# Pairing the transposes of a sparse attention's steps and grouping the value products of two memory attentions

## The chip, the core and the metric

The kernel runs on one core of a Trainium2 chip. The metric is device time in microseconds (us), from the first to the last instruction of one execution, as the median of several runs. Five engines work side by side, each through its own queue in order: TensorE (PE; its weight loads are shown apart as PEld), VectorE (DVE), ScalarE (ACT), GpSimd (POOL) and SyncE (SP), which here only issues DMAs. TensorE's results land in PSUM, which this kernel uses as eight banks of 128 x 512 floats; VectorE and ScalarE copy them out.

## What is computed

The reference is a two-layer trunk on one sequence of 512 tokens and width 1024, all in fp32. Layer 0 mixes tokens by a gated linear attention (GLA), layer 1 by a sparse attention (NSA) with three branches: compressed keys, selected blocks, and a window. In both layers a *memory attention* over 256 memory tokens runs beside it, and both are followed by an output projection and a feed-forward network with a short convolution. Cut to what matters here:

```python
def mem_attention(q, mem_kv):                       # 4 heads of 64, 256 memory tokens
    s = einsum("bshd,bmhd->bhsm", qh, kh) * 64 ** -0.5
    return einsum("bhsm,bmhd->bshd", softmax(s), vh)

def nsa_mixer(q, gates, shared, rel_bias):          # 12 heads of 64 in 4 groups
    p_c = masked_softmax(q @ kc.T + bias)           # compressed keys, 31 of them
    o_c = p_c @ vc
    o_s = masked_softmax(q @ k_sel.T + bias) @ v_sel    # selected blocks: all 8 blocks here
    o_w = masked_softmax(q @ kw.T + bias) @ vw          # window of 512
    return g0 * o_c + g1 * o_s + g2 * o_w
```

With 512 tokens there are 8 blocks of 64 and up to 16 may be selected, so the selected branch is causal attention over the whole sequence, like the window.

## The kernel before, in words

Every fp32 product that needs full precision is made of three one-pass products: an operand is split into a high part (ScalarE rounds it to fp32r) and a low part (VectorE subtracts), and high x high, low x high and high x low are summed in PSUM. TensorE's stream is nearly without gaps. A framework places the instructions: each engine's queue follows the program's order, except where an instruction would wait by its own estimate and a later one is free to go first. Where the order matters it is written out by hand: `behind` (L239) ties one instruction behind another on its engine, and in the sparse attention `pe` (L1714) chains all of the stage's matmuls and transposes in program order; only matmuls from outside this chain, such as the output projection's, can still come between.

PSUM is handed out in four pairs of banks, "acc", "sc", "pt" and "po" (`ps`, L209).

**The memory attention** (`mem_att`, L497) works on two pairs of heads, m = 0 and 1, and four tiles of 128 tokens. Ten iterations: iteration i computes the scores of pair and tile i (`scores`, for i under 8), and transposes the weights of i - 2 (`turn`, L521: for each head of the pair two transposes into a "pt" bank, then a copy to the tile mPT, by ScalarE for the first head and VectorE for the second). `fill` puts matmuls of other work in between. When a pair's four tiles are turned, `out` (L534) computes its value products: eight fp32 matmuls of 128 x 64 weights on 512 columns, two heads side by side on the two halves of TensorE's columns, into a "pt" bank, which is then split into mo. Pair 0's products stand in iteration 6, between its scores and its turn (L555), with the split tied between the turn's two copies; pair 1's come after the last iteration (L559).

**The sparse attention** (`nsa_layer`, L1555) has twelve steps: six pairs of heads a = 0..5 (head a with head a + 6), and for each the tiles (0, 3) and then (1, 2) of 128 queries. What belongs to a step:

- `scores` (L1771): for each of the two heads three parts of two matmuls. VectorE adds the bias and takes the minimum, ScalarE exponentiates into the tile P, and after the third part GpSimd multiplies P by gate over sum.
- `copies` (L1889): a DMA from SP's queue copies the finished P to R, from where TensorE reads it in one pass. P and R have three buffers each.
- `weights_t` (L1901): six parts, three for each head. A part is 2 to 4 transposes of R into one bank (mostly "pt", the second branch of a large tile into "acc" up to step 7) and one copy to PT, by ScalarE or VectorE.
- `values` (L1921): 20 fp32 matmuls of PT with V, two heads side by side on half the columns each, into a "po" bank; after tile 2 two more on full columns add the compressed branch, from its transposed weights PcT.
- `compressed` (L1805): the compressed branch for a pair of heads, in four portions: scores on half columns and softmax, multiplication by the gate, transposes of Pc with the copies to PcT.
- `project` (L1724): the query projection of pair a + 2, 24 matmuls, two for each slot of two steps; there is none from step 8 on.

The loop at the end runs over the steps, and each step has six slots (`for i in range(6)`, L1958). A slot s, i issues: a part of the scores of step s + 1, one part of the transposes (half a step behind, so the first three slots finish step s - 1 and the others begin step s), the copies that are due, and two matmuls of the projection. Slot 3 of the even steps 2 to 10 adds, ahead of that: the last portion of the compressed branch (Pc's transposes), the next one's first portion, and the values of the two steps before. Step 11 has no scores and no projection.

Of the kernel before, what the change touches and what calls it, by code (L numbers as in the profile page):

```python
# [18 lines left out]
S = 512  # L19
# [163 lines left out]
class Trunk:  # L183
# [313 lines left out]
    def mem_att(self, qfs, pool, mK, mV, mo, first, fill, qpool, direct=False):  # L497

        nc = self.nc
        Q, P, PT = {}, {}, {}  # L500

        def scores(m, qt):
            ts = slice(128 * qt, 128 * qt + 128)
            sc = self.ps("sc")
            for hh in range(2):
                for i in range(2):
                    ins = nc.tensor.matmul(sc[:, MEM * hh:MEM * hh + MEM], Q[m][hh][i][:, ts], mK[2 * m + hh], start=i == 0, stop=i == 1)
                    if direct:
                        self.behind(ins, self.last)
            mn = self.t(self.small, [128, 2], "mmn")  # L510
            nc.vector.tensor_reduce(out=mn, in_=sc.rearrange("p (h k) -> p h k", h=2), op=ALU.min, axis=AX.X)
            p = P[m, qt] = self.t(pool, [128, 2, MEM], "mP", bufs=3)
            sm = self.t(self.small, [128, 2], "msm")
            for hh in range(2):
                nc.scalar.activation(p[:, hh, :], sc[:, MEM * hh:MEM * hh + MEM], AF.Exp, bias=mn[:, hh:hh + 1], scale=-1.0,
                                     accum_out=sm[:, hh:hh + 1])
            nc.vector.reciprocal(sm, sm)
            for hh in range(2):
                nc.vector.tensor_scalar_mul(p[:, hh, :], p[:, hh, :], sm[:, hh:hh + 1])

        def turn(m, qt, between=None):  # L521
            ts = slice(128 * qt, 128 * qt + 128)
            if qt == 0:
                PT[m] = [self.t(pool, [128, 2, S], f"mPT{hh}", bufs=1) for hh in range(2)]
            for hh in range(2):
                pt = self.ps("pt")
                for kt in range(2):
                    nc.tensor.transpose(pt[:, 128 * kt:128 * kt + 128], P[m, qt][:, hh, 128 * kt:128 * kt + 128], self.ident)
                eng = nc.vector.tensor_copy if hh else nc.scalar.copy
                ins = eng(PT[m][hh][:, :, ts], pt[:, :256].rearrange("p (k t) -> p k t", k=2))  # L530
                if between and hh == 0:
                    between(ins)

        def out(m):  # L534

            po = self.ps("pt")
            for kt in range(2):
                for hh in range(2):
                    g = 2 * m + hh
                    nc.tensor.matmul(po[64 * hh:64 * hh + 64, :], mV[:, kt, 64 * g:64 * g + 64], PT[m][hh][:, kt, :], start=kt == 0, stop=kt == 1)  # L540
            def parts(after=None):
                self.split_to(mo[m][0], mo[m][1], po)
                if after is not None:
                    self.behind(self.made, after)

            return parts

        Q[0] = self.stack_q(qfs[0], pool, qpool, direct)
        first()
        for i in range(10):  # L550
            if i < 8:
                scores(*divmod(i, 4))
            if i == 3:
                Q[1] = self.stack_q(qfs[1], pool, qpool)
            between = out(0) if i == 6 else None  # L555
            if i >= 2:
                turn(*divmod(i - 2, 4), between)
            fill()
        out(1)()  # L559


    def gla_layer(self):
# [992 lines left out]
    def nsa_layer(self):  # L1555
        nc, I, tc = self.nc, self.I, self.tc
        with ExitStack() as outer:
            pool = outer.enter_context(tc.tile_pool(name="nsa", bufs=1))
# [10 lines left out]
            with tc.tile_pool(name="nsap", bufs=2) as pp:  # L1569
# [70 lines left out]
                for j in range(2):  # L1640
# [44 lines left out]
                    else:  # L1685
# [7 lines left out]
                        for g in range(4):  # L1693
                            hh = g // 2
# [29 lines left out]
            def project(a):  # L1724

                wh, wl = self.wget(self.W["nsaq"][a], GMIX)
                ps = self.ps("acc")
                for k in range(KC):
                    ws = slice(128 * k, 128 * k + 128)
                    xh, xl = self.x[k]  # L1730
                    for i, (u, w) in enumerate(((wh, xh), (wl, xh), (wh, xl))):
                        mm(ps, u[:, ws], w, start=k + i == 0, stop=k == KC - 1 and i == 2)
                        if k < KC - 1 or i < 2:
                            yield
                qfs_[a] = self.t(qp, [128, S], "qf", bufs=2)
                nc.vector.scalar_tensor_tensor(out=qfs_[a], in0=ps, scalar=-0.125, in1=rb, op0=ALU.mult, op1=ALU.mult)
                yield
# [101 lines left out]
            run = lambda g, n=1: [next(g, None) for _ in range(n)]  # L1839

            with ExitStack() as ms:
# [6 lines left out]
                def values():  # L1848
                    pv = [self.ps("acc" if t < 2 else "po") for t in range(4)]
                    yield from self.stepsB("nsav", 0, 2, 512, pv, self.x, GKV)  # L1850
                    for t in range(4):
                        nc.scalar.activation(V[:, t], pv[t].rearrange("p (a d) -> p a d", d=64), AF.Copy, scale=rc[:, t:t + 1])
# [30 lines left out]
            with tc.tile_pool(name="nsac", bufs=2) as cp:  # L1883
# [5 lines left out]
                def copies():  # L1889

                    while scaled:
                        s, hh, flat = scaled.pop(0)
                        a, qts = steps[s]
                        direct = s == 11 and hh == 1
                        R = flat if direct else self.t(cp, [128, 1280], "R", FR, bufs=3)
                        for sp, t in zip(spans[qts], qts):
                            if not direct:
                                nc.sync.dma_start(R[:, sp].bitcast(F32), flat[:, sp])
                            Ps[a, t, hh] = by_branch(R[:, sp]), F32 if direct else FR
# [45 lines left out]
                def turns():  # L1945
                    for s in range(12):
                        yield from weights_t(s)

                copies()
                now = turns()  # L1950
                main = [None] * 6 + mo
                for s, (a, qts) in enumerate(steps):
                    ahead = scores(s + 1) if s < 11 else iter(())
                    if qts[0] == 0:
                        proj = project(a + 2) if a < 4 else iter(())
                        q = queries(a + 1) if a < 5 else iter(())
                        run(q)
                    for i in range(6):  # L1958
                        if i == 3 and s and not qts[0]:
                            run(c)  # L1960
                            c = compressed(a)
                            run(c)
                            run(values(s - 2))
                            run(values(s - 1))
                        if i == 4 and s == 11:
                            run(c)
                            run(values(10))
                        if a < 5 and i in (3, 4) and not qts[0]:
                            run(q)
                        if i == 5 and s and not qts[0]:  # L1970
                            run(c)
                        if a < 5 and not i and qts[0]:
                            run(q, 2)
                        run(ahead)
                        if s or i > 2:
                            run(now)
                        copies()
                        run(proj, 2)
                    if 8 <= s < 11:
                        main[s - 8] = self.split(o[s - 8], self.xp, [128, S], "x")  # L1980
                        self.behind(self.made, turned[True])
                        self.behind(self.left, turned[False])
                run(now, 3)
                run(values(11))
            self.w_out(1, main)

# [25 lines left out]
```

## Time and profile before

| | before |
|---|---|
| median of 3 runs (lowest to highest) | 1220.11 us (1219.74 to 1221.58) |
| the profiled execution | 1219.85 us, span 1218.1 us |
| instructions | 22021, of these 8321 matmuls |
| memory attention of layer 0, last fill to last products | up to about 111 us |
| memory attention of layer 1 | up to about 706 us |
| loop of the sparse attention | about 709 to 824 us |

A line of the profile names the line of the kernel, the engine, the operation, out<-in by the program's names, shapes and count; in a timeline the first number is the start in us from the start of the span and the second how long it was busy. TensorE's rows overlap, since its matmuls are pipelined, so their cost is read from start to start. `idle before <-X` names what an engine waited for.

### The profile page before, as it was taken

The page shows a single profiled execution, that of the slowest core. Times are in us where ns is not written, and L with a number is a line of the kernel's source. Part 1 is how long each engine was busy: PE and PEld are TensorE (multiplying, and loading weights), DVE is VectorE, ACT ScalarE, POOL GpSimd, SP SyncE. Part 2 cuts the span into 40 slices and gives each one's busy share as a digit, 9 for nine tenths or more (in the row PEclk, how much of TensorE's full clock was granted, in tenths as well). Part 3 has the DMA queues.
Part 4 walks back from the last instruction along what each step waited for, and adds up shares of the span by engine and source line. Part 5 has one row for each costly group of instructions (what it writes and reads, how often), then busy time and mean ns, then how long its engine had stood idle before and what let it go on. Part 6 is the DMA issues. An engine that isn't in the chain of part 4 may idle for free.

```text
span 1218.1 us, 22021 instructions
## 1 busy us (share of the span) xinstructions
PE 1209.1 (99%) x8321; PEld 1077.6 (88%) x8321; DVE 916.3 (75%) x1637; ACT 729.9 (60%) x1459; POOL 271.0 (22%) x290
## 2 busy tenths in 40 slices
PE   9999999999999999999999999999999999999998
PEld 8887889889999998888888888888899999998887
DVE  7667886698888889644776788975788888889431
ACT  8656655467666667333545678763576666685331
POOL 1000000014444420000003265650034444400000
PEclk9999999999999999999999999999999999999999
DMA  7541013236666642322725467733256666633221
GB/s 263 156 139 60 36 37 105 102 104 171 158 158 156 156 124 90 122 92 98 223 105 173 115 227 249 234 116 121 81 141 160 156 157 156 157 105 108 104 70 69
DMA packets 59776, 163.09 MB, mean 134 GB/s; under 512 B 7309, under 2 KB 13384, under 8 KB 59670
## 3 DMA queue, kind: packets, MB, share of 16 engines
q1 hardware_dynamic: 47638, 140.66, 34.1%
q0 software_dynamic: 10944, 19.93, 10.8%
q8 instruction: 65, 1.06, 0.4%
q10 hardware_dynamic: 1088, 1.10, 0.3%
q14 instruction: 41, 0.34, 0.1%
HBM read 116.13 MB, written 2.15 MB: 97 GB/s over the span
## 4 chain that ended last, share of the span: by engine, by line
PE 92%; DVE 2%; POOL 2%; issue 2%; ACT 1%; DMA 1%; SPq 0%; POOLq 0%; DVEq 0%; ACTq 0%
PE pt L1190 18%; PE acc L326 10%; PE po L1190 9%; PE acc L1423 7%; PE acc L1007 6%; PE po L1362 5%; PE sc L1362 5%; PE sc L1190 5%; PE po L346 3%; PE acc L793 3%; PE po L1721 2%; PE acc L1486 2%; PE acc L1721 2%; PE acc L1627 2%; PE acc L346 2%
## 5 line engine op out<-in xcount | busy, mean ns | idle before, releaser
L287 ACT ACTIVATE wh<-wraw 128x1024 fp32r<-128x1024 f32 (+1 forms) x105 | 109.3, 1042 | 138.9 <-PE sc L1362 29.6
L288 DVE TENSOR_TENSOR wl<-wraw,wh 128x1024 fp32r<-128x1024 f32 (+1 forms) x105 | 130.7, 1246 | 74.2 <-ACT wh L287 73.4
L1179 DVE TENSOR_TENSOR wl<-wraw,wh 128x1024 fp32r<-128x1024 f32 x76 | 72.6, 955 | 7.4 <-ACT wh L1176 7.4
L326 PE MATMUL acc<-xh,wh 128*128 128x512 f32 x184 | 72.6, 394 | 0.0
L326 PE MATMUL acc<-xl,wh 128*128 128x512 f32 x184 | 71.9, 391 | 0.0
L326 PE MATMUL acc<-xh,wl 128*128 128x512 f32 x184 | 71.9, 391 | 0.0
L1423 PE MATMUL acc<-a,wh 128*128 128x512 f32 x228 | 71.2, 389 | 0.0
L1170 POOL DMA_DIRECT2D wraw<-rbw x38 | 33.4, 879 | 154.4 <-DVE wl L1179 111.0
L1179 DVE TENSOR_TENSOR wl<-rbw,wh 128x1024 fp32r<-128x1024 f32 x38 | 46.5, 1225 | 25.9 <-ACT wh L1176 25.9
L1176 ACT ACTIVATE wh<-wraw 128x1024 fp32r<-128x1024 f32 x76 | 63.9, 844 | 1.2 <-DMA wraw<-rbw 1.2
L1060 DVE SCALAR_TENSOR_TENSOR hc<-acc,ntap,hc 128x511 f32<-128x511 f32 x76 | 56.9, 749 | 10.1 <-ACT hc L1057 8.2
L1801 POOL TENSOR_TENSOR P<-P,ssm 128x256 f32<-128x256 f32 (+3 forms) x48 | 61.7, 1306 | 1.9
L1060 DVE SCALAR_TENSOR_TENSOR hc<-acc,vec,hc 128x511 f32<-128x511 f32 x76 | 56.9, 749 | 2.9 <-ACT hc L1057 1.7
L1793 ACT ACTIVATE P<-P,smn 128x128 f32<-128x128 f32 (+3 forms) x96 | 53.3, 557 | 6.5 <-DVE smn L1791 3.2
L1362 PE MATMUL po<-a,wh 128*128 128x512 f32 x144 | 56.0, 389 | 0.0
L1362 PE MATMUL sc<-a,wh 128*128 128x512 f32 x144 | 56.0, 389 | 0.0
L1165 POOL TENSOR_TENSOR rbw<-s,rbw 128x512 f32<-128x512 f32 x36 | 47.8, 1329 | 36.7 <-DVE xh L1068 19.0
L1176 ACT ACTIVATE wh<-rbw 128x1024 fp32r<-128x1024 f32 x38 | 40.3, 1059 | 22.8 <-issue 19.7
L1423 PEld LDWEIGHTS acc<-a,wh 128*128 128x128 f32 x228 | 42.8, 188 | 8.9
L1176 ACT ACTIVATE wh<-s 128x512 fp32r<-128x512 f32 x38 | 24.0, 632 | 42.4 <-PE pt L1190 42.4
L1159 POOL TENSOR_TENSOR s<-wraw,rbw 128x512 f32<-128x512 f32 x34 | 44.8, 1316 | 20.2 <-DVE wl L1179 20.2
L1423 PE MATMUL acc<-a,wl 128*128 128x512 f32 x114 | 44.3, 389 | 0.0
(726 smaller groups left out, 4330.4 us busy)
## 6 DMA issues: line engine op xcount, KB each, us to landing
wraw<-in_wp SPq DMA_DIRECT2D x156, 512.0 KB, 3.2
rbw<-in_wp SPq DMA_DIRECT2D x38, 512.0 KB, 4.4
rbw<-rbw POOLq DMA_DIRECT2D x38, 256.0 KB, 4.2
wraw<-rbw POOLq DMA_DIRECT2D x38, 256.0 KB, 3.3
R<-P SPq DMA_DIRECT2D x12, 512.0 KB, 3.3
strip<-vecd SPq DMA_DIRECT2D x12, 448.0 KB, 4.8
R<-P SPq DMA_DIRECT2D x11, 384.0 KB, 3.0
qd<-qf SPq DMA_DIRECT2D x24, 128.0 KB, 3.2
```

The costliest lines, as they stand in the source:

```text
L287: self.made = nc.scalar.activation(wh, raw, AF.Copy)
L288: self.left = nc.vector.tensor_tensor(out=wl, in0=raw, in1=wh.bitcast(F32), op=ALU.subtract)
L326: self.last = self.nc.tensor.matmul(ps[:M, :N], u[:, M * k:M * k + M], x[k][i][:, :N], start=n == 0, stop=n == 23)
L346: self.last = nc.tensor.matmul(ps[:, :N], s_, m_, start=k == 0 and n == 0, stop=k == KC - 1 and n == 2)
L1007: self.nc.tensor.matmul(ps[:, cols], a[:, o], b[:, cols], start=start and i == 0 and k == ks[0], stop=stop and k == 5 and i == 2)
L1060: return [nc.vector.scalar_tensor_tensor(out=c[:, 2 - i:], in0=u[:, :S - 2 + i], scalar=tap(half, j, i, neg), in1=c[:, 2 - i:], op0=ALU.mu ...
L1176: return after("A", nc.scalar.activation(out, x, AF.Copy))
L1179: return after("D", nc.vector.tensor_tensor(out=out, in0=x, in1=hi.bitcast(F32), op=ALU.subtract))
L1190: after("P", nc.tensor.matmul(bank[:, :256], w[:, o], x, start=start and k + i == 0, stop=k == 3 and i == 2, skip_group_check=True))
L1362: after("P", nc.tensor.matmul(first[m], a[:, o], x, start=r + i == 0, stop=r == NJ - 1 and i == 2))
L1423: nc.tensor.matmul(ps, a[:, o], x, start=n == 0, stop=n == 3 * NJ - 1)
L1801: nc.gpsimd.tensor_tensor(out=P, in0=P, in1=f[:, i, :].unsqueeze(2).to_broadcast([128, 2, 128 * t + 128]), op=ALU.mult)
```

## The change

In `mem_att` the products of pair 0 are taken out of iteration 6 and put behind the last iteration, ahead of those of pair 1; then both are split. The tile mPT gets two buffers, since both pairs are now kept to the end.

In the loop of the sparse attention:

- the transposes run two parts at a time, in the slots 0, 2 and 4 (in step 0 only slot 4; in step 11 also slot 5) instead of one part in every slot, so two are left for the end instead of three;
- in slot 3 of the even steps the values of step s - 2 go ahead of the compressed branch's portions, instead of behind them, and in step 11 those of step 10 do;
- the copies from P to R are not issued in the last slot of a step any more but in the first of the next.

```diff
-                PT[m] = [self.t(pool, [128, 2, S], f"mPT{hh}", bufs=1) for hh in range(2)]
+                PT[m] = [self.t(pool, [128, 2, S], f"mPT{hh}", bufs=2) for hh in range(2)]
...
-            between = out(0) if i == 6 else None
             if i >= 2:
-                turn(*divmod(i - 2, 4), between)
+                turn(*divmod(i - 2, 4))
             fill()
-        out(1)()
+        for part in [out(m) for m in range(2)]:
+            part()
...
                         if i == 3 and s and not qts[0]:
+                            run(values(s - 2))
                             run(c)
                             c = compressed(a)
                             run(c)
-                            run(values(s - 2))
                             run(values(s - 1))
                         if i == 4 and s == 11:
+                            run(values(10))
                             run(c)
-                            run(values(10))
...
                         run(ahead)
-                        if s or i > 2:
-                            run(now)
-                        copies()
+                        if i in (0, 2, 4) and (s or i > 2) or i == 5 and s == 11:
+                            run(now, 2)
+                        if i < 5:
+                            copies()
                         run(proj, 2)
...
-                run(now, 3)
+                run(now, 2)
                 run(values(11))
```

## The prediction, made before the changed kernel was run

> **What bounds the kernel now.** I read the page first (busy shares, slices, the chain), then busy time by stage, then TensorE's rows in order of time around the two places that the diff edits, and last who TensorE waited for in the sparse attention.
>
> ```profile
> span 1218.1 us, 22021 instructions
> PE 1209.1 (99%) x8321; PEld 1077.6 (88%) x8321; DVE 916.3 (75%) x1637; ACT 729.9 (60%) x1459; POOL 271.0 (22%) x290
> ```
>
> TensorE is busy for 1209.1 of 1218.1 us. A time saved on another engine is worth nothing unless TensorE waits for it; a time saved or added in TensorE's own stream counts in full. In the sparse attention the other engines are close behind:
>
> ```profile
> 724.00:744.00 20.00, 19.61 (x186) 16.89 (x183) 17.01 (x52) 15.31 (x47) 11.80 (x17) 1.00 0.73 249
> 783.00:804.00 21.00, 20.39 (x190) 16.93 (x188) 19.37 (x57) 17.11 (x53) 12.86 (x17) 1.00 0.63 210
> ```
>
> The columns are length, then busy PE, PEld, DVE, ACT, POOL, granted clock (1.00), DMA share, GB/s. In the later stage, where no projection runs any more, VectorE is busy for 19.37 of 21 us. So work that bunches there can make TensorE wait. It waits little today (window 705 to 826):
>
> ```profile
> PE sc L1721 <- DVE smn L1791: 0.5, 1, 0.5
> PE acc L1721 <- ACT PT L1917: 0.4, 1, 0.4
> PE pt L1722 <- ACT PT L1917: 0.2, 1, 0.2
> PE acc L1007 <- ACT xh L301: 0.2, 1, 0.2
> ```
>
> That is 1.3 us, and the most that the waits listed there can give back. The sum is made against the profiled execution, 1219.85 us (1.75 us of it outside the span of 1218.1); the median of the runs shown, 1220.11, is 0.26 higher.
>
> **Part 1: two parts of a step in one run of transposes.** A part is 2 to 4 transposes between scores and two projection matmuls. What does a run cost?
>
> ```profile
> 733.93 0.40 PE L1721 MATMUL sc<-K,Ql 128*128 128x512 f32 x1
> 734.16 0.46 PE L1722 MATMUL pt<-ident,R 128*128 128x128 f32 x4
> 734.46 0.47 PE L1721 MATMUL acc<-xl,wh 128*128 128x512 f32 x1
> 734.77 0.39 PE L1721 MATMUL acc<-xh,wh 128*128 128x512 f32 x1
> ...
> 819.55 0.45 PE L1722 MATMUL pt<-ident,R 128*128 128x128 f32 x3
> 819.84 0.43 PE L1722 MATMUL sc<-ident,R 128*128 128x128 f32 x3
> 820.10 1.08 PE L1722 MATMUL pt<-ident,P 128*128 128x128 f32 x7
> ```
>
> Starts count, not busy times, which overlap. A run of four holds TensorE from 734.16 to 734.46, 0.30 us, and the matmul behind it takes 0.31 (734.46 to 734.77) where a 512-column matmul takes 0.23 (733.93 to 734.16): 0.61 in all, of which 0.08 is lost behind the run. One would save that 0.08 with each pair joined, if the transposes kept their pace. They do not: in the one long run of before the second three take 0.26 (819.84 to 820.10), 0.087 each, against 0.30 / 4 = 0.075 in the run of four. Joined, four and four cost 0.61 + 4 x 0.087 = 0.96, and the matmul that lost its run 0.23: 1.19, against 2 x 0.61 = 1.22. The gain is 0.03 us a pair, 0.02 if the rows' rounding falls the other way.
>
> How many pairs: up to the loop's step 10 there are 63 parts in 63 runs now (three in step 0, six in each of the next ten) and 62 parts in 31 runs after. In step 11 no scores or projection stand between the parts, so nothing is joined that wasn't next to each other. 31 pairs x 0.02 to 0.03 give 0.6 to 0.9 us; I take **-0.8 us**.
>
> **Part 2: one group of value products in each memory attention.** The products of pair 0 now stand between the scores and the turns of iteration 6. First the GLA layer's iterations 5 and 6, then the other layer's:
>
> ```profile
> 93.93 0.28 PE L507 MATMUL sc<-mK,Qh 128*128 128x256 f32 x1
> ...
> 96.91 0.28 PE L507 MATMUL sc<-mK,Qh 128*128 128x256 f32 x1
> 97.03 0.28 PE L507 MATMUL sc<-mK,Ql 128*128 128x256 f32 x1
> 97.14 0.28 PE L507 MATMUL sc<-mK,Qh 128*128 128x256 f32 x1
> 97.27 0.28 PE L507 MATMUL sc<-mK,Ql 128*128 128x256 f32 x1
> 97.47 1.94 PE L540 MATMUL pt<-mPT,mV 128*64 128x512 f32 x8
> ...
> 102.27 0.28 PE L507 MATMUL sc<-mK,Qh 128*128 128x256 f32 x1
> ...
> 681.72 0.28 PE L507 MATMUL sc<-mK,Qh 128*128 128x256 f32 x1
> ...
> 685.38 0.28 PE L507 MATMUL sc<-mK,Qh 128*128 128x256 f32 x1
> ...
> 691.13 0.28 PE L507 MATMUL sc<-mK,Qh 128*128 128x256 f32 x1
> ```
>
> ```profile
> 97.96 0.14 PEld L540 LDWEIGHTS pt<-mPT,mV 128*64 128x64 f32 x2 [0.29 <-issue]
> 98.39 0.14 PEld L540 LDWEIGHTS pt<-mPT,mV 128*64 128x64 f32 x2 [0.29 <-issue]
> ```
>
> The products go in pairs of half the array's columns, a pair every 0.43 us (97.96 to 98.39), so four pairs are worth 1.72. Iteration 6 is longer than iteration 5 by (102.27 - 96.91) - (96.91 - 93.93) = 5.36 - 2.98 = 2.38 us in the first layer, and by 5.75 - 3.66 = 2.09 in the second, with the same filling matmuls. What goes beyond 1.72 is 0.66 and 0.37: the price of going into the half-array products and out again, and of a turn that finds one of its two banks taken. At the end of the attention pair 1 stands in such a group already; pair 0, put in front of it, pays 1.72 and no second way in and out. That is **-1.03 us**. The two splits of pair 0 move to the end with it; the first of them runs while pair 1's products take their 1.72 us, and the larger PT buffer is no instruction. If that cover is gone, the splits delay the next stage's use of the banks by some tenths.
>
> **Part 3: step values ahead of the compressed branch.** This edit is easily read as a mere exchange. In the steps 2, 4, 6, 8 and 10, now: Pc transposes, compressed scores, products of step s-2, products of step s-1, all but the transposes on half arrays. After: products of s-2, Pc transposes, compressed scores, products of s-1. TensorE goes into the half-array form twice where it went once.
>
> ```profile
> 745.09 4.54 PE L1721 MATMUL po<-PT,V 128*64 128x128 f32 x80
> 749.56 0.74 PE L1721 MATMUL po<-PcT,vcz 128*128 128x512 f32 x2
> ...
> 817.21 2.41 PE L1721 MATMUL po<-PT,V 128*64 128x128 f32 x40
> ```
>
> Going in costs 0.20 instead of 0.12 (97.27 to 97.47 against 97.03, 97.14, 97.27): 0.08. Eighty rows that follow other half-array work take 4.47 with one way out, forty with a way in and a way out 2.34 (817.21 to 819.55), 0.105 more than half, which is half a way out and a slow first pair: with 0.1 for the way out (estimated from the 0.08 of the way in) 0.05 for the pair, 0.15 together. The three transposes behind take 0.29 where three take 0.26: 0.03. Sum 0.26; part 2 gave 0.37 for the cheaper of its two stays. I take 0.30 x 5 = **+1.5 us**, with 1.3 and 1.9 as ends.
>
> The Trainium skill, "TensorEngine Tiling (Array Packing)", section "Key Properties", says that a change of tiling mode, not of tile alone, drains TensorE; this speaks against part 3 and for part 2, and the rows agree that something is paid at each change. "TensorE: Matmul & The Clock Gate", section "Single matmul latency", puts a drain at about 175 ns, and by that estimate a stay costs 0.35 and the sum would come 0.2 us higher; the rows above show about 0.1 at each change with the rest on the matmuls behind.
>
> **What costs nothing.** The copies to R of the last slot go out one slot later, past the next step's queries and strips on SP's queue; they are used a whole step (six slots of some 1.2 us, and more with the products) later, and wait for GpSimd's scaling anyway. In step 11 the products of step 10 go ahead of the compressed branch with as many ways in and out as before. Without that slack a copy would be late by one slot, about 1.2 us, once.
>
> **Waits.** Two copies out of a run now follow each other on ScalarE and VectorE. Below, the gain is bounded by 2.2 us; above, by the two slower rivals. I take 0: all engines do the same work, and the copies have their step's length to be read.
>
> Sum: -0.8 - 1.03 + 1.5 = -0.33 us, so 1219.85 - 0.33 = 1219.5 for the profiled execution and 1219.8 by the median. 0.2%, 2.4 us, is about what a measurement of this kernel can tell from no change (its three runs lie 1.84 apart). **The forecast is no change that can be told.** Chance 0.57.
>
> **Rivals.** *Slower: the compressed branch's transposed weights come late.* Between the Pc transposes and the products with vcz only one step's products are left as cover.
>
> ```profile
> 723.23 0.60 PE L1722 MATMUL pt<-ident,Pc 128*64 128x128 f32 x4
> 727.07 0.69 DVE L1836 TENSOR_TENSOR PcT<-pt,PcT 64x512 fp32r<-64x512 f32 x1
> 728.75 0.73 PE L1721 MATMUL po<-PcT,vcz 128*128 128x512 f32 x2
> ...
> 804.23 0.60 PE L1722 MATMUL pt<-ident,Pc 128*64 128x128 f32 x4
> ```
>
> ```profile
> 806.16 0.68 DVE L1836 TENSOR_TENSOR PcT<-pt,PcT 64x512 fp32r<-64x512 f32 x1
> ```
>
> Cover now: 723.23 to 728.75, 5.52 us; after, less half of 4.47: 3.3. PcT was there 4.53 us after the transposes began in step 2 (727.07 + 0.69) and 2.61 in step 10. If VectorE's lag stays, step 2 would wait 1.2, step 10 not; with 0.6 as the mean, five steps cost 3.0, and the sum is +2.7: 1222.8. It decides from a lag over 3.3. For it: both engines run behind TensorE here. Against it: the lag is a queue of scores and copies, and the products now put ahead give it 2.2 us to drain; with a drained queue, as in step 10, PcT is in time. Chance 0.15.
>
> *Slower: a bank comes back too late.* With pairs, the bank of part 0 is wanted by part 3 two slots later instead of three.
>
> ```profile
> 736.29 0.28 PE L1721 MATMUL sc<-K,Qh 128*128 128x256 f32 x1
> 736.52 0.46 PE L1722 MATMUL pt<-ident,R 128*128 128x128 f32 x4
> ...
> 739.76 0.40 PE L1721 MATMUL sc<-K,Qh 128*128 128x512 f32 x1
> ```
>
> ```profile
> 738.75 0.66 DVE L1917 COPY PT<-pt 128x512 f32<-128x512 f32 x1
> ```
>
> Three slots take 3.47 us (736.29 to 739.76), two 2.3, and with part 2's transposes ahead 2.6; VectorE had that bank copied 2.9 after its transposes began (738.75 + 0.66 - 736.52). 0.3 short in each of some ten steps: +3, in all 1222.8. Against it: this is one of the longest lags, and a step that waits once lets the copies catch up. Chance 0.07.
>
> *Faster: the waits go.* The pairs leave every second slot without a turn, and the two engines may catch up there. Besides the 1.3 listed, the three turns of step 11 that follow within 4 us may lose less to the banks, for which I allow 0.9. Then -0.33 - 2.2 = -2.5: 1217.6. For it: the waits stand at copies out of banks. Against it: VectorE's 19.37 of 21 us do not shrink. Chance 0.17.
>
> *The change does not do what it says.* Only TensorE's chain of this stage is written out by hand; w_out's matmuls fill gaps from step 8 on and can still part a pair. A third of the pairs undone costs 0.3 us: still no change. Chance 0.04.
>
> **How the numbers follow.** Faster by over 0.2%: the faster rival (0.17) and 0.02 of the forecast's tail, 0.19. Slower: 0.22 of the two rivals less the half of their outcomes below 1222.5 (0.07), and 0.04 of the forecast's tail, 0.19. The rest, 0.62, within 0.2%. The forecast's own range is 1218.5 to 1221.5; that of 8 in 10 reaches into the rivals, 1217.2 to 1222.8.
>
> **What would show it.** Right: in the changed trace runs of six to eight transposes at about 0.087 each, one matmul of 0.30 behind each run; the memory attentions' products x16 in one row, and the iterations 6 of equal length with the others; products x40 on both sides of the Pc transposes, each with 0.2 before its first row. Wrong: TensorE idle ahead of po<-PcT with VectorE's PcT as releaser (first rival), idle ahead of pt<-R with PT copies as releaser (second), or fewer than 0.5 us of listed waits (third). A run of eight at 0.06 each would overturn part 1.

## The result, and the profile after

The changed kernel takes 1227.24 us (median of 6 runs, 1227.0 to 1229.25); the kernel before took 1221.54 beside it (6 runs, 1219.74 to 1221.78). The ratio is 1.0054, with a 95% interval of 1.0044 to 1.0064: slower by half a per cent. The forecast, 1219.8 and no change, was wrong.

The page of the changed kernel (its profiled execution took 1227.06 us):

```profile
span 1225.3 us, 22032 instructions
PE 1211.8 (99%) x8321; PEld 1080.4 (88%) x8321; DVE 917.8 (75%) x1637; ACT 730.4 (60%) x1459; POOL 278.7 (23%) x290
```

The span grew by 7.2 us, TensorE's busy time by 2.7 only, VectorE's by 1.5 and GpSimd's by 7.7, although all of them run the same work. So one looks for waits first: who TensorE waited for in the sparse attention (window 690 to 840).

```profile
PE sc L1721 <- DVE smn L1791: 2.0, 1, 2.0
PE pt L1722 <- ACT PT L1917: 1.6, 3, 0.7
PE sc L1721 <- DVE Ql L302: 0.8, 1, 0.8
PE acc L1007 <- ACT xh L301: 0.7, 1, 0.7
PE acc L1722 <- ACT PT L1917: 0.3, 2, 0.2
PE po L1721 <- DVE PcT L1836: 0.2, 1, 0.2
```

5.6 us, where the list of before had 1.3. (smn is VectorE's minimum over a part of the scores, taken by the instruction that empties the bank of scores; Ql is VectorE's subtraction that makes the low part of a query.) The longest wait has a consequence that no list of waits shows. The same stretch by windows (length, then busy PE, PEld, DVE, ACT, POOL, granted clock, DMA share, GB/s):

```profile
792.00:796.00 4.00, 2.74 (x16) 2.09 (x16) 2.99 (x8) 1.08 (x3) 2.06 (x4) 1.00 0.76 268
796.00:800.00 4.00, 3.25 (x16) 2.66 (x17) 3.75 (x17) 4.00 (x13) 1.60 (x4) 0.79 0.76 244
800.00:804.00 4.00, 4.00 (x23) 3.36 (x21) 4.00 (x5) 2.57 (x9) 2.35 (x2) 0.78 0.30 115
804.00:808.00 4.00, 4.00 (x28) 3.24 (x26) 3.77 (x16) 3.88 (x14) 2.67 (x3) 1.00 0.23 83
```

Behind the wait TensorE's clock is granted at 0.79 and 0.78 of full speed over four us each: (0.21 + 0.22) x 4 = 1.7 us lost. In this execution the waits beyond those of before and the clock are together 4.3 + 1.7 = 6.0 of the 7.2. What the slow clock is worth in the median is not shown: another of the six executions had a mean granted clock of 0.999 (0.997 in the profiled one, 0.998 to 1.0 in those of the kernel before) and took 1227.0 us all the same. Where the long wait comes from stands in VectorE's rows of that place, step 8:

```profile
789.73 1.35 DVE L302 TENSOR_TENSOR Ql<-qd,Qh 128x512 fp32r<-128x512 f32 x1 [0.72 <-ACT Qh L301]
791.11 0.68 DVE L1836 TENSOR_TENSOR PcT<-pt,PcT 64x512 fp32r<-64x512 f32 x1
791.82 0.66 DVE L1817 TENSOR_TENSOR Pc<-sc,strip 128x124 f32<-128x124 f32 x2
792.52 0.41 DVE L1820 TENSOR_REDUCE cmn<-Pc 128x8 f32<-128x248 f32 x1
792.96 0.99 DVE L1821 TENSOR_TENSOR Pc<-Pc,cmn 128x248 f32<-128x248 f32 x1
794.90 0.42 DVE L1826 TENSOR_REDUCE cf<-Pc 128x8 f32<-128x256 f32 x1 [0.94 <-POOL Pc L1824]
795.23 0.42 DVE L1791 CUSTOM_DVE_ANT_0 P<-sc,strip 128x256 f32<-128x256 f32 x1
```

TensorE issued the scores for that last row at 792.41. VectorE was then still at the compressed branch, whose sum cf has to wait for ScalarE's exponential and GpSimd's mask, and the row that would free the "sc" bank stands behind cf in VectorE's queue: it starts 2.82 us after its scores. In the kernel before the same row started 1.53 after them (790.79, scores at 789.26):

```profile
790.19 0.42 DVE L1826 TENSOR_REDUCE cf<-Pc 128x8 f32<-128x256 f32 x1 [0.27 <-POOL Pc L1824]
790.64 0.20 DVE L1827 RECIPROCAL cf<-cf 128x8 f32<-128x8 f32 x1
790.79 0.42 DVE L1791 CUSTOM_DVE_ANT_0 P<-sc,strip 128x256 f32<-128x256 f32 x1
```

Two durations in the changed rows are odd as well: Ql at 1.35 us, where all ten took 0.68 to 0.76 before, and Pc<-Pc,cmn at 0.99, where the same instruction took 1.65 before.

### The profile page after: what moved, and what is told of

It is laid out like the page before. It is cut to its first block, busy times and chain, and to the rows that moved or that the text cites. A ratio compares the mean times of both kernels' runs of the same rounds, so it can differ in the third digit from the quotient of the medians.

```text
span 1225.3 us, 22032 instructions
## 1 busy us (share of the span) xinstructions
PE 1211.8 (99%) x8321; PEld 1080.4 (88%) x8321; DVE 917.8 (75%) x1637; ACT 730.4 (60%) x1459; POOL 278.7 (23%) x290
## 4 chain that ended last, share of the span: by engine, by line
PE 94%; DVE 2%; ACT 2%; issue 1%; DMA 0%; POOL 0%; SPq 0%; POOLq 0%; DVEq 0%; ACTq 0%
PE pt L1190 18%; PE acc L326 11%; PE po L1190 9%; PE acc L1423 7%; PE acc L1007 6%; PE po L1362 5%; PE sc L1362 5%; PE sc L1190 5%; PE po L346 3%; PE acc L793 3%; PE po L1721 2%; PE acc L1486 2%; PE acc L346 2%; PE acc L1627 2%; PE acc L1721 2%; PE sc L1007 1%
## 5 line engine op out<-in xcount | busy, mean ns | idle before, releaser
L1801 POOL TENSOR_TENSOR P<-P,ssm 128x256 f32<-128x256 f32 (+3 forms) x48 | 67.2, 1420 | 1.9
```

The costliest lines, as they stand in the source:

```text
L1801: nc.gpsimd.tensor_tensor(out=P, in0=P, in1=f[:, i, :].unsqueeze(2).to_broadcast([128, 2, 128 * t + 128]), op=ALU.mult)
```

## The experiments

Two theories to begin with. *Late branch*: the new order of slot 3 starts the next compressed branch later and does the harm. *Bunched copies*: two copies out of banks in a row hold TensorE. Times are medians, and ratios are to the kernel before, measured beside each of four groups of experiments (its medians were 1220.67, 1220.83, 1221.07 and 1221.09).

### The parts of the change, one by one

The memory attentions' edit alone (its lines of the diff above, nothing in the loop):

```diff
-            between = out(0) if i == 6 else None
...
+        for part in [out(m) for m in range(2)]:
+            part()
```

> The memory attentions' edit alone. Both theories, late branch and bunched copies, leave this part as I priced it: about 1.0 us faster than before, between 0.6 and 1.3. If it is not faster, the priced way in and out of the half-array products is wrong, or something behind the attention pays it back.

1220.09 us, ratio 0.9994 (0.9985 to 1.0003): 0.6 less, at the lower end of what was expected, and not to be told from no change.

The pairs with the moved copies, in the old order of slot 3:

```diff
-                        if s or i > 2:
-                            run(now)
-                        copies()
+                        if i in (0, 2, 4) and (s or i > 2) or i == 5 and s == 11:
+                            run(now, 2)
+                        if i < 5:
+                            copies()
...
```

> The turns in pairs with the copies of the last slot issued one slot later; slot 3 in its old order. Late branch (the order of slot 3 does the harm): between 0.8 us faster and 0.8 us slower than before, no halved clock. Bunched copies (two PT copies in a row hold banks too long): at least 4 us slower, with waits on PT copies ahead of transposes in most steps.

1227.96 us, ratio 1.0061 (1.0048 to 1.0073).

The new order of slot 3 and step 11 alone:

```diff
+                            run(values(s - 2))
                             run(c)
                             c = compressed(a)
                             run(c)
-                            run(values(s - 2))
...
```

> The order of slot 3 (and of step 11) alone, one part of the transposes in each slot as before. Late branch: 4 to 7 us slower than before, 1.5 of it the five extra stays in half-array form, the rest TensorE waiting for VectorE behind the compressed branch, with a stretch of halved clock. Bunched copies: 1.5 us slower, from the stays alone, and no new wait.

1225.25 us, ratio 1.004 (1.0028 to 1.0053). The time is in the range of *late branch*, but its stretch of halved clock isn't there: every window of this stage is granted full clock. The waits that are new in its list are spread: 0.8 us for Ql, 0.7 for PcT, 0.3 for cf.

The changed kernel without the new order (the first two edits together):

```diff
-                            run(values(s - 2))
                             run(c)
                             c = compressed(a)
                             run(c)
+                            run(values(s - 2))
...
```

> The whole change without the new order of slot 3 and step 11. Late branch: 0.2 to 1.8 us faster than before, at least 5 us faster than the changed kernel. Bunched copies: 3 us or more slower than before. If the two edits add, it is the sum of the two runs that have one of them each.

1226.15 us, ratio 1.0045 (1.0032 to 1.0057).

The memory attentions are innocent. The pairs alone cost 7.3, the order alone 4.6, all of it together about 6. Costs of TensorE's own work would add; waits can cover each other. Neither theory can be the whole: *late branch* had nothing for the pairs, *bunched copies* only 1.5 for the order. In the kernel with the pairs alone, TensorE waits for other things (window 690 to 840; its first four rows):

```profile
PE sc L1721 <- DVE Ql L302: 2.1, 2, 1.2
PE sc L1721 <- ACT PT L1917: 1.0, 1, 1.0
PE pt L1722 <- DVE ssm L1795: 0.8, 1, 0.8
PE acc L1007 <- ACT xh L301: 0.7, 1, 0.7
```

Ql is qd - Qh. All rows of it (minimum, median, maximum in ns), first in the kernel before, then with the pairs:

```profile
L302 DVE TENSOR_TENSOR Ql<-qd,Qh x10: 678/691/761, 709.8 to 795.2; 128x512 fp32r<-128x512 f32 x10
```

```profile
L302 DVE TENSOR_TENSOR Ql<-qd,Qh x10: 691/1084/1952, 710.3 to 801.3; 128x512 fp32r<-128x512 f32 x10
```

And GpSimd at the place of the longest, 801.34 (1.95 us):

```profile
799.82 2.92 POOL L1801 TENSOR_TENSOR P<-P,ssm 128x512 f32<-128x512 f32 x2
```

The subtraction ends at 803.29, 0.55 after GpSimd's scaling of P ended at 802.74. It looks held until the scaling is over. That gave a third theory, *held subtractions*: a VectorE instruction with both inputs in SBUF, and GpSimd's scaling of P, hold each other.

The Trainium skill, "SBUF — State Buffer", section "SBUF: two separate sides", says just this: VectorE and GpSimd share a pair of ports, an instruction of VectorE with two SBUF inputs needs it, and the loser waits for the whole instruction of the other. The runs with a short scaling, below, agree: every Ql takes 0.68 to 0.72 us there, and every Pc<-Pc,cmn 0.41 to 0.42.

### Copies, and GpSimd's scaling cut short

The pairs with the copies to R issued in every slot again:

```diff
-                        if i < 5:
-                            copies()
+                        copies()
```

> The pairs alone, on the kernel before, with the copies to R issued in all six slots as before. Theory 'held subtractions': VectorE's subtractions with both inputs in SBUF (Ql, xl) take 0.69 us when GpSimd is idle and up to 1.95 when its scaling of P runs, since the two hold each other; the pairs shift VectorE against GpSimd, and the copies to R are not the cause: 1225 to 1228. Theory 'late copies': the copies of slot 5, a slot late, keep a P buffer taken and VectorE waits for it (1.88 us in step 1 of the pairs with moved copies, 0.43 before): with them in slot 5 again the loss goes, 1220 to 1222. Theory 'bunched copies': two copies out of banks in a row hold TensorE: as with the moved copies, 1227 to 1228.

1228.07 us, ratio 1.0051 (1.0037 to 1.0064), as slow as with the moved copies. These cost nothing, as forecast, and *late copies* falls.

The kernel before, with GpSimd scaling only 8 columns of each part of P, which leaves out most of the scaling; VectorE's, ScalarE's and TensorE's instructions keep their order. A kernel with this edit is called its *short form*:

```diff
-nc.gpsimd.tensor_tensor(out=P, in0=P, in1=f[:, i, :].unsqueeze(2).to_broadcast([128, 2, 128 * t + 128]), op=ALU.mult)
+nc.gpsimd.tensor_tensor(out=P[:, :, :8], in0=P[:, :, :8], in1=f[:, i, :].unsqueeze(2).to_broadcast([128, 2, 8]), op=ALU.mult)
```

> The kernel before, with GpSimd scaling only the first 8 columns of each part of P instead of all 128 to 512 (the remaining weights are left unscaled); every other instruction is in its old order. It is the base for the next two. All theories: little of GpSimd's time is on the path of the kernel before (1.5 us of waits in this stage): 1219 to 1221. Held subtractions would show all Ql, xl and Pc subtractions at their short times, 0.69 and 0.42 us.

1219.43 us, ratio 0.9986 (0.9977 to 0.9994). The five subtractions Pc<-Pc,cmn, first with full and then with short scaling:

```profile
L1821 DVE TENSOR_TENSOR Pc<-Pc,cmn x5: 1561/1648/1667, 727.8 to 807.3; 128x248 f32<-128x248 f32 x5
```

```profile
L1821 DVE TENSOR_TENSOR Pc<-Pc,cmn x5: 417/418/420, 727.9 to 806.7; 128x248 f32<-128x248 f32 x5
```

So the kernel before was held too, 5 x 1.23 = 6.2 us of VectorE's time, at a place where TensorE was not waiting for it. In the changed kernel four of these five are free (0.42) and the holding falls on Ql, which TensorE waits for (0.8 us in its list):

```profile
L302 DVE TENSOR_TENSOR Ql<-qd,Qh x10: 654/933/1951, 708.4 to 800.9; 128x512 fp32r<-128x512 f32 x10
```

The changed kernel and the pairs with the same edit:

```diff
-nc.gpsimd.tensor_tensor(out=P, in0=P, ...
+nc.gpsimd.tensor_tensor(out=P[:, :, :8], in0=P[:, :, :8], ...
```

> The changed kernel with the same short scaling. Held subtractions: what is left of the change is TensorE's own pace (stays in half-array form +1.5 to +2, pairs 0 to -0.8, memory attentions -1) and some waits at copies, so at most 2.5 over the short form of the kernel before: 1219.5 to 1222.5. Bunched copies: the waits at PT copies (2.6 us) and their consequences stay: 4 or more over it, 1223.5 to 1227. Late branch: the compressed branch's chain still comes late and TensorE waits about 2 us behind it in step 8: 3 or more over it.

> The pairs with the moved copies (1227.96 with full scaling), with the same short scaling. Held subtractions: of the 7.3 us at most 2 are left over the short form of the kernel before: 1219 to 1222. Bunched copies: 5 or more are left: 1225 to 1228.

The changed kernel: 1223.57 us, 4.1 over the short form of before (ratio 1.0017, 1.0009 to 1.0026, to the kernel before itself). The pairs: 1221.59, 2.2 over it (1.0008, 0.9999 to 1.0016). In the pairs with short scaling every Ql is short again:

```profile
L302 DVE TENSOR_TENSOR Ql<-qd,Qh x10: 681/690/702, 710.7 to 796.8; 128x512 fp32r<-128x512 f32 x10
```

GpSimd's long scalings are behind 5.1 of the pairs' 7.3 us, and behind some 2 of the changed kernel's 6. The edit takes away two things at once, the holding and the time for which cf and the weights queue behind the scalings on GpSimd, so the 5.1 is the price of both. In the pairs *bunched copies* missed (5 or more left was expected, 2.2 were left). In the changed kernel *held subtractions* missed (at most 2.5 left was expected, 4.1 were left): something else is there.

### Late banks

The kernel before and the pairs again, and now with the copies out of the banks cut short too, to 8 columns each (PT's other columns stay zero, by four memsets that aren't shown). These are the *light forms*:

```diff
-                                copied = eng(PT[:, brs[0]:brs[-1] + 1, :], pt[...])
+                                copied = eng(PT[:, brs[0]:brs[-1] + 1, :8], pt[...][:, :, :8])
...
```

> The kernel before with the short scaling and with copies of transposed weights out of the banks of only the first 8 columns of each part (the other columns of PT stay zero, four memsets more on GpSimd). The base for the next one. Copies hold TensorE for 0.5 us at most in the kernel with the short scaling alone (1219.43): 1218 to 1220.

> The pairs with moved copies, with the same short scaling and short copies. What is left is TensorE's own pace. Theory 'late banks' (the second part of a run finds its bank still waiting for its copy; of the 2.2 us that the pairs cost over the short form, all is this): the 40 transposes between two compressed branches go from 3.3 to 3.6 us to 3.15, and the pairs gain what was forecast, 0.4 to 0.8 us, against the light form of the kernel before: 1217.3 to 1219.5. Theory 'slow transposes' (a long run is slow in itself): the transposes stay above 3.3 us and the pairs stay 1.5 to 2.5 slower than the light form.

1217.77 us for the light form of before (ratio 0.9971, 0.9961 to 0.9982), 1217.5 for the pairs (0.997, 0.9959 to 0.9982): the pairs' last 2.2 us are gone. The 0.3 us that they are ahead is less than *late banks* expected and can't be told from nothing. The edit also takes time off ScalarE and VectorE, which do the copies, so the price of late banks isn't separated from that. One run, in slot 2 of step 4, first in the pairs with short scaling and full copies, then in the light pairs:

```profile
744.57 0.37 PE L1722 MATMUL pt<-ident,R 128*128 128x128 f32 x3
745.10 0.45 PE L1722 MATMUL acc<-ident,R 128*128 128x128 f32 x3 [0.16 <-ACT PT L1917]
745.38 0.47 PE L1721 MATMUL acc<-xh,wl 128*128 128x512 f32 x1
```

```profile
743.39 0.37 PE L1722 MATMUL pt<-ident,R 128*128 128x128 f32 x3
743.61 0.46 PE L1722 MATMUL acc<-ident,R 128*128 128x128 f32 x3
743.90 0.46 PE L1721 MATMUL acc<-xh,wl 128*128 128x512 f32 x1
```

The run takes 0.81 us instead of 0.51, and only 0.16 of these 0.30 is listed as a wait: the first three transposes are shown as busy for 0.37, although the next part starts 0.22 behind them where it needn't wait. Waits of this kind are found from start to start, not in the list. The same run loses 0.3 us in the steps 2 and 6 too. The copy it waits for, on ScalarE of the first of the two kernels:

```profile
743.60 0.50 ACT L1793 ACTIVATE P<-P,smn 128x256 f32<-128x256 f32 x1
744.10 0.50 ACT L1793 ACTIVATE P<-P,smn 128x256 f32<-128x256 f32 x1
744.59 0.46 ACT L1917 COPY PT<-acc 128x384 f32<-128x384 f32 x1
```

It empties the "acc" bank of the run that began at 742.19, 2.4 us after its start, since it stands behind exponentials.

With full scaling more runs are late. The one in slot 0 of step 5 takes 1.04 us in the pairs (755.93 to 756.97), but 0.46 with short scaling alone (755.33 to 755.79). In the pairs its copy stands behind three exponentials, the first of which had itself to wait; below, that exponential and the wait of the transposes:

```profile
754.76 0.51 ACT L1793 ACTIVATE P<-P,smn 128x256 f32<-128x256 f32 x1 [1.38 <-DMA R<-P]
...
756.77 0.37 PE L1722 MATMUL pt<-ident,R 128*128 128x128 f32 x2 [0.38 <-ACT PT L1917]
```

So late banks are in the 5.1 us of the short scaling as well.

### The late branch

cf and what follows it on VectorE tied behind the two score parts that come next after the branch's block (the fourth and fifth part of the next step), in the changed kernel:

```diff
-                                nc.vector.tensor_tensor_reduce(out=P[:, br, :n], ...
+                                self.scored = nc.vector.tensor_tensor_reduce(out=P[:, br, :n], ...
...
-                nc.vector.tensor_reduce(out=f, in_=Pv, op=ALU.add, axis=AX.X)
+                self.behind(nc.vector.tensor_reduce(out=f, in_=Pv, op=ALU.add, axis=AX.X), self.scored)
```

> The changed kernel, with one order more: in each compressed branch the sum over Pc (cf) and what follows it on VectorE stands behind the first two score parts of the next step instead of ahead of them. In step 8 of the changed kernel VectorE waits for GpSimd ahead of cf, the scores wait behind it, TensorE waits 2.0 us and then runs 3.4 us at half clock. Theory 'late branch': the wait and the slow clock go, 3 us or so less: 1223 to 1225. Theory 'held subtractions alone': the Ql ahead of it is held all the same and the wait only changes its name: 1226 to 1228.

1223.93 us, ratio 1.0021 (1.0013 to 1.003): 3.3 less than the changed kernel. The long wait is shorter, and no window of this stage is granted less than full clock:

```profile
793.82 0.36 PE L1721 MATMUL sc<-K,Qh 128*128 128x256 f32 x1 [1.35 <-DVE smn L1791]
```

The order alone with short scaling (the edit of before's short form), and with the tie and full scaling (the edit just shown):

```diff
+                            run(values(s - 2))
                             run(c)
...
-nc.gpsimd.tensor_tensor(out=P, in0=P, ...
+nc.gpsimd.tensor_tensor(out=P[:, :, :8], in0=P[:, :, :8], ...
```

> The new order of slot 3 and step 11 alone, with GpSimd's short scaling; base is the short form of the kernel before, 1219.43. The block of products, Pc transposes and compressed scores took 6.27 us in the new order against 6.08, so five blocks are worth 0.95. Theory 'late branch': besides that, the compressed branch's chain starts 2.2 us later on VectorE and its cf holds the next scores: 1221.4 to 1223. Theory 'held subtractions': without GpSimd's long scalings nothing but the 0.95 is left: 1220.2 to 1220.8.

> The new order alone, full scaling, with cf tied behind the first two score parts (the order alone took 1225.25, 4.6 over the kernel before). Late branch: the tie takes 1.5 to 3 of it, 1222 to 1223.8. Held subtractions alone: the loss stays, 1224.5 to 1226.

1222.74 us with short scaling (ratio 1.0016, 1.0007 to 1.0025), 3.3 over the short form of before: GpSimd's scalings are only the smaller part of the order's loss. 1222.29 with the tie (ratio 1.0011, 1.0002 to 1.002), 3.0 less than without. Both as *late branch* had it. What is left of the order's cost then is 1.2.

The tie in the old order, alone and with the memory attentions' edit:

```diff
...
+                self.behind(nc.vector.tensor_reduce(out=f, in_=Pv, op=ALU.add, axis=AX.X), self.scored)
...
```

> The kernel before with nothing but the tie of cf. The tie with the memory attentions' edit took 1219.05, the edit alone 1220.09. If the two add: 1219.3 to 1220.0, and the edit is worth 0.5 to 1 with the tie as well. If the tie is worth nothing by itself: 1220.5 to 1221.2.

> The kernel before with the memory attentions' edit alone, and the same tie of cf behind the first score parts. If a late cf holds the scores in the old order too (0.47 us of wait in step 8, 0.1 to 0.3 in others): 0.3 to 0.8 less than the memory edit alone, 1219.3 to 1219.8. If cf is not on the path there: 1220.0 to 1220.6.

1220.33 us alone (ratio 0.9995, 0.9986 to 1.0004) and 1219.05 with the edit (0.9984, 0.9975 to 0.9993). The second beats both kernels, by 2.0 us on the kernel before, a little more than was expected; the wait of 0.5 us for smn is no longer in its list. The tie alone cannot be told from no change.

### What is left without waits

The whole change with short scaling, short copies and the tie:

```diff
+                self.behind(nc.vector.tensor_reduce(out=f, in_=Pv, op=ALU.add, axis=AX.X), self.scored)
...
+nc.gpsimd.tensor_tensor(out=P[:, :, :8], in0=P[:, :, :8], ...
...
+                                copied = eng(PT[:, brs[0]:brs[-1] + 1, :8], pt[...][:, :, :8])
```

> The whole change with every wait taken off as far as can be: short scaling, short copies, cf tied. Against the light form of the kernel before (1217.77) only TensorE's own pace should be left: memory attentions -0.7 to -0.9, pairs -0.3 to -0.8, blocks +0.95. Theory 'only waits were missed': 1217.0 to 1218.0. If some cost of TensorE's own was missed as well (a slower run, a slower way into the half-array form): 1218.8 or more.

1218.18 us (ratio 0.9975, 0.9967 to 0.9984), 0.4 over the light form of before, from which it can't be told, and just above the range of *only waits were missed*. Its list of waits is empty from 690 to 840, so its rows show TensorE's own pace. From one compressed branch's block to the next, first in the light form of before, then in the light pairs, then in the light whole:

```profile
723.70 0.60 PE L1722 MATMUL pt<-ident,Pc 128*64 128x128 f32 x4
...
743.72 0.60 PE L1722 MATMUL pt<-ident,Pc 128*64 128x128 f32 x4
```

```profile
724.39 0.60 PE L1722 MATMUL pt<-ident,Pc 128*64 128x128 f32 x4
...
744.43 0.60 PE L1722 MATMUL pt<-ident,Pc 128*64 128x128 f32 x4
```

```profile
722.33 2.40 PE L1721 MATMUL po<-PT,V 128*64 128x128 f32 x40
...
742.68 2.40 PE L1721 MATMUL po<-PT,V 128*64 128x128 f32 x40
```

20.02, 20.04 and 20.35 us: here the pairs gain nothing, and the new order costs 0.31. In the next cycle it is 20.04, 20.03 and 20.30.

## Why the prediction was wrong, point by point

- **Part 1, the pairs' own pace: forecast -0.8, measured -0.3 by the medians of the light forms, whose intervals overlap, and 0 by the rows.** The mechanism was right (fewer matmuls behind runs, slower transposes in long runs); summed over the rows of the first of these cycles, the 40 transposes took 3.26 us instead of 2.82, and the matmuls behind runs gave back about 0.40. The few hundredths by which the one was to exceed the other are not there.
- **Part 2, the memory attentions: forecast -1.03, measured -0.95 in the trace.** From the scores of iteration 5 to the matmul behind the products the first took 17.13 us (93.93 to 111.06) and now 16.30 (94.05 to 110.35), 0.83 less where 0.66 was forecast. The second took 24.56 (681.72 to 706.28) and now 24.44 (680.99 to 705.43), 0.12 less where 0.37 was forecast. That the sum fits better than its two terms is luck, and by the medians of the edit alone it is 0.6. The products now stand in one row:

```profile
106.76 3.65 PE L540 MATMUL pt<-mPT,mV 128*64 128x512 f32 x16
110.35 0.70 PE L824 MATMUL sc<-lev,la 128*96 128x512 f32 x2
```

- **Part 3, the stays in half-array form: forecast 0.30 each, measured 0.31.** That the order costs TensorE's own time was right, and the size too. That TensorE leaves the half-array form for the Pc transposes, as the prediction says, isn't shown: their rows say 128*64, as those of the products do. So the 0.31 is the price of the order, whatever the form. By the estimate of 0.35 from the Trainium skill's drain of 175 ns ("TensorE: Matmul & The Clock Gate", section "Single matmul latency") five stays would cost 0.2 more; the rows stand with the smaller price.
- **What costs nothing: right for the copies to R** (with and without the move 1227.96 and 1228.07).
- **Waits: this is the step that failed.** "I take 0: all engines do the same work, and the copies have their step's length to be read." They do the same work at other times, and here that was worth about 6 us: in the profiled execution 4.3 us more of listed waits and 1.7 of slow clock behind one of them. Three chains make it up, and they overlap: the tie takes off 3.3 of the whole change, the short scaling takes 5.1 off the pairs alone, the short copies 2.4 more. (Shown by runs; how much of the 5.1 is holding and how much is GpSimd's queue, and how much of the 2.4 is late banks and how much the shorter copies, isn't separated.)
- **The rivals.** *Bank back too late* fits what the light forms showed, 2.4 us against the 3 that were worked out, and it was given 0.07. Its sign, TensorE idle ahead of pt<-R with PT's copies as releaser, stands in the changed kernel's list with 1.6 us. What was held against it, that a step that waits once lets the copies catch up, fails because the copies stand behind ScalarE's exponentials, which can be late themselves (one waited for 1.38 us in the row above). *PcT late* was looked at on the wrong side of the move: PcT kept TensorE waiting for 0.2 us, once, and for 0.7, once, with the order alone. The order does not only shorten the cover of the branch that is finished, it starts the next branch's scores 2.2 us later while the score parts behind them come as early as ever, and the long chain VectorE, ScalarE, GpSimd, VectorE up to cf then holds them. That chain was in the diff (both portions of the branch are moved) and was not followed.
- **VectorE's 19.37 busy of 21 us** was read as work. At least 2.1 of it was holding: Pc<-Pc,cmn took 1.65 us there and wl<-wraw,wh 2.12, and with short scaling they take 0.42 and 1.22. Such holding can move to where it hurts.

## What to carry to other kernels

When TensorE is full and the other engines are close behind, moving work in TensorE's order without changing its amount still shifts every other queue: for each moved step, follow the chain that it starts on the other engines to its last instruction, and see what is queued behind that one. An instruction whose rows differ in duration for one shape may be waiting inside, as Ql and Pc were here: find with what it overlaps before the busy share is taken for load. A gain of hundredths of a microsecond a place, from a queue within tenths of its cover, is not worth the move.

## What the runs showed of the hardware

- VectorE subtractions of two SBUF operands (128x512) took 0.68 to 0.76 us in the kernel before and up to 1.95 beside GpSimd's scaling, those of Pc (128x248) 0.42 with short scaling and up to 1.67 beside the full one. GpSimd seems to be held in its turn: its busy time rose by 7.7 us in the changed kernel, and 5.5 of this is the same 48 scalings of P (67.2 us instead of 61.7). VectorE's copies out of a bank, 128x512 from PSUM, stayed at 0.65 to 0.69 in the kernel before, the changed kernel and the pairs.
- Behind 2.0 us without a matmul TensorE ran at a lower granted clock (0.79 and 0.78 over two windows of 4 us, 1.7 us lost; 0.50 in every half microsecond from 798.5 to 801.5). A single wait of 1.35 us had no such consequence in the changed kernel with the tie. It takes no single long wait, though: in the kernel with the memory attentions' edit and the pairs, the granted clock was 0.58 from 820 to 824, behind two waits of 0.5 and 0.7 us close together. So the first of these waits cost 3.7 us in all, nearly twice its length.
